# A hybrid attention and state-space layer on one core: a lead before some attention jobs, tables issued sooner, a bank for K0, splits moved to VectorE, gelu in another order and a gated unit with the contraction outside

## The chip, the cores and the metric

The kernel runs on one core of one Trainium2 chip. The metric is the time of one execution on the device in microseconds (us), the median of several runs. A profiled execution gives the trace, from which every row below comes.

## The reference, cut to what matters

One decoder layer over 2048 tokens of width 1024, in float32:

```python
proj = x @ w_in                               # q, k, v, z_a, u, z_s, gate logits
# attention: three groups (window, dilation) = (128,1), (512,4), (2048,16), 8 slots of 64
s = q @ k.T / 8 + alibi; m = s.max(-1); p = exp(s - m); l = p.sum(-1); o = p @ v / l
attn = sum(l * exp(m - m_all) * o) / sum(l * exp(m - m_all)) * silu(z_a)
# state space: 32 groups of 16 channels, 64 complex states each, a scan over the tokens
bu = bb @ u; x_t = ab * x_{t-1} + bu; y = gelu(Re(c @ x_t) + d * u)
y = y * sigmoid(y @ w_glu + b_glu) * silu(z_s)
out = (sigmoid(g_a) * (attn @ w_attn_up) + sigmoid(g_s) * (y @ w_ssm_up)) @ w_o
return layer_norm(2 ** 0.25 * x + out)
```

The output has to be float32 in quality, so each product is made of three: an operand is split in a high half (a rounded copy) and a low half (the rest), and TensorE adds high x high, high x low and low x high.

## The kernel before, in words

Work is written as Python generators that yield after every few matmuls, and the order in which they issue instructions is the order of each engine's queue. `interleave` (L237) mixes a bulk generator (projections, 48 products of 512 columns a block, `BLK`) with a side generator (tables, an attention job, the state-space stage): it takes the side whenever its share of its own total is no larger than the bulk's share. TensorE thus always has bulk products between the side's steps.

The tokens go in two halves of 1024 (h = 0, 1). The stages are:

1. Prologue: the projection of u, then V, Q and K of the first attention job, beside `s5_tables` (L735), some hundreds of small VectorE instructions. Their yields add up to 25.01; the side total given is 29.0, the bulk's is 8 blocks. It ends with five stores of the tables from SP (L926, L928).
2. For each half, four head pairs and three groups: `job_proj` (L346) makes Q, K (and V for even pairs, `v_gemm` L403) and `job_attn` (L519) does the attention of the job before it as the side. Odd pairs have another projection (`za` or `zs`) behind K. Q and K come out of PSUM as two copies of ScalarE (L382) and two subtractions of VectorE (L384). V goes through DRAM: ScalarE stores it, SP loads it (L370), ScalarE copies the high half (L375, issued inside K's product), POOL subtracts (L376). For the third group, the keys of every token block lie in both halves of K's product. The first step of `job_attn` is a bias (L525, VectorE) and `scores(0)`, two products of the two slots (L579) and two more with the low half of Q (L581).
3. The gates (16 for each half, `gate_block` L683, `tanh` by ScalarE at L703) beside `s5` (L984), whose side total is `S5_TOTAL` = 340. For every 4 groups, `setup` builds E and F (VectorE, with two products on POOL, L1012 and L1017), K0 = E x F (L1030, bank `sca`), copies it (L1033, ScalarE), stores it and loads it shifted as MD (L1034, L1043). For every 2 groups, `part_a` (L1087, bank `sca`) makes the scan's input, which ScalarE copies to BR and BI (L1094, L1095; two buffers), `part_b` is the scan, 38 VectorE instructions (L1106 to L1134), and `part_c` (L1153, L1154, bank `scb`) makes y, which goes to DRAM.
4. `yprep` (L1193) loads y of half 1 channel by channel and applies gelu: Square (ScalarE, L1207), a product (VectorE, L1209), Tanh (ScalarE, L1211), a product (L1213), the high half (ScalarE, L1217), the low half (VectorE, L1219), for four blocks, as the last part of the side.
5. `stage_glu` (L1225) multiplies y by w_glu, one output block after another, each in one bank for 512 tokens; the eviction is a tanh (ScalarE, L1240), two products and a low half (VectorE, L1244, L1245, L1252). Then `stage_y`, `stage_c` and the norm, with half 0's gelu beside `stage_c` of half 1.

Weights: `Weights` (L124) has a plan of 128x1024 tiles in the order of use and two raw buffers. `ahead` (two contraction steps into a product) begins the next tile's split: the high half of one 512-column part by ScalarE (L171), the low half by POOL (L172). `ahead2` (six steps in) does the other part and fetches the tile after. The evictions of one product and the start of the next are ordered by the two `proj` banks.

Of the kernel before, what the change touches and what calls it, by code (L numbers as in the profile page):

```python
# [9 lines left out]
F32 = mybir.dt.float32  # L10
F32R = mybir.dt.float32r
# [8 lines left out]
HALF = 1024  # L20
# [21 lines left out]
def layer_kernel(ctx, tc, xT, xnat, w_in, w_v, w_up, w_glu, w_o, bglu, lng, lnb,  # L42
# [81 lines left out]
    class Weights:  # L124
        def __init__(self, plan):
            self.plan, self.raws, self.splits, self.i = plan, [], [], 0
            self.open = False

        def fetch(self, upto):
            while len(self.raws) < min(upto, len(self.plan)):  # L130
# [35 lines left out]
        def part(self, k, i=None):  # L166
            i = len(self.splits) - 1 if i is None else i
            hi, lo = self.splits[i]
            raw = self.raws[i][0]
            c = self.cols(i, k)  # L170
            A.copy(hi[:, c], raw[:, c])  # L171
            (V if i < 2 and not k else P).tensor_tensor(lo[:, c], raw[:, c], hi[:, c].bitcast(F32), op=OP.subtract)  # L172
            self.open = k == 0

        def finish(self):
            if self.open:
# [2 lines left out]
        def take(self):  # L179
            self.split(self.i + 1)  # L180
            self.finish()
            self.i += 1
            return self.splits[self.i - 1]

# [9 lines left out]
    def gemm(wts, nkt, mh, ml, evac, outer=False, w=None, k0=0, banks=None):  # L194
        hi, lo = w or wts.take()
        last = 3 * nkt - 1
        lead = k0 == 0

        def mms(ps, t, kt):
            cols = slice(t * 512, (t + 1) * 512)  # L200
            wc = slice((k0 + kt) * 128, (k0 + kt + 1) * 128)
            for n, (w, m) in enumerate(((hi, mh), (hi, ml), (lo, mh))):
                T.matmul(ps, w[:, wc], m(kt)[:, cols], start=kt == 0 and n == 0, stop=3 * kt + n == last)  # L203

        if outer:
            ps = [ps_tile(*(banks[t] if banks else ("proj", 2))) for t in range(2)]
            for kt in range(nkt):
                for t in range(2):
                    mms(ps[t], t, kt)
                if kt == 1:  # L210
                    wts.ahead()
                if kt == min(5, nkt - 1):
                    wts.ahead2()
                yield 6 * 0.216
            for t in range(2):
                evac(t, ps[t])
            return
        for t in range(2):
            ps = ps_tile("proj", 2)
            for kt in range(nkt):  # L220
                mms(ps, t, kt)
                if kt % 2 == 1:
                    if t == 0 and kt == 1 and lead:
                        wts.ahead()
                    if t == 0 and kt == min(5, nkt - 1) and lead:
                        wts.ahead2()
                    if kt < nkt - 1:
                        yield 6 * 0.216
            evac(t, ps)
            yield 6 * 0.216  # L230
# [3 lines left out]
        return gemm(wts, 8, lambda k: X["h", k], lambda k: X["l", k], evac, outer, banks=banks)  # L234


    def interleave(bulk, bulk_total, side, side_total):  # L237
        b = s = 0.0
        bulk_on = side_on = True
        while bulk_on or side_on:  # L240
            if side_on and (not bulk_on or s / side_total <= b / bulk_total):
                try:
                    s += next(side)
                except StopIteration:
                    side_on = False
            else:
                try:
                    b += next(bulk)
                except StopIteration:
                    bulk_on = False  # L250
# [469 lines left out]
    glu = [w_glu[e] for e in range(2)]  # L720
    up = [w_up[d] for d in range(8)]
    fin_o = [w_o[q, k] for q in range(2) for k in range(4)]
    plan += gate + gate + (glu + up + fin_o) * 2
    wts = Weights(plan)

    def drain(g):
        for _ in g:
# [3 lines left out]


    G = 32

    def s5_tables(sp):  # L735
        yield 0.01
# [183 lines left out]
                 ks[:, :, n, 0], ks[:, :, n, 1], tk)  # L920
        ts(ks[:, :, :, 2], ks[:, :, :, 1], -1.0, OP.mult)

        o = 0
        for t in (Q1, Q2, P1, P2):
            n = t.shape[1] * t.shape[2]
            S.dma_start(tabD[:, o:o + n], t.rearrange("s g k -> s (g k)"))  # L926
            o += n
        S.dma_start(tabD[:, o:], ks.rearrange("s g n w -> s (g n w)"))  # L928

    def s5_views(sp):  # L930
        tab = sp.tile([128, 1472], F32, name="tab")
# [6 lines left out]
    with tc.tile_pool(name="ap", bufs=1) as ap:  # L938
        ub = [u_block(0, b) for b in range(2, 4)]
        interleave(chain([first_blocks(first_x(ap), [u_evac(0, b) for b in range(2)])] + ub  # L940
                         + [job_proj(ap, wts, 0, 0, 0)]), 8 * BLK, s5_tables(ap), 29.0)
        pend = None
        for h in range(2):
            bulk = [u_block(1, b, b == 0) for b in range(4)] if h else []
            n = len(bulk)
            for pair in range(NPAIR):
                for g in range(3):
                    if h or pair or g:
                        bulk.append(job_proj(ap, wts, h, pair, g))
                        n += 2 if pair % 2 else 4  # L950
                    if pair % 2:
                        bulk.append(zs_block(h, pair // 2) if g == 1 else za_block(h, pair - 1 + g // 2))
                        n += 1
                    if pend is None:
                        drain(chain(bulk))
                    else:
                        interleave(chain(bulk), n * BLK, pend, 16.0)
                    pend = job_attn(ap, jobs.pop())
                    bulk, n = [], 0
            if h == 0:  # L960
                raws = []
                for tag, n in (("QA", 1), ("QB", 1), ("cB", 1), ("KC", 2), ("VV", 2), ("og", 1)):
                    t = ap.tile([128, n * HALF], F32, name="xr", tag=tag, bufs={"og": 5, "cB": 1}.get(tag, 2))
                    raws += [t[:, HALF * k:HALF * k + HALF] for k in range(n)]
                part = iter_until(pend, 3.0)
                zs = [zs_block(0, b, b == 3 and "last") for b in range(2, 4)]
                interleave(chain([spread(zs[0], lambda k: S.dma_start(raws[k], xT[1, k]), 1), next_x(1, zs[1], raws)]),
                           1.2 * BLK, part, 3.0)

        def tail():  # L970
            yield from pend
            while fins:
                step_fin()
                yield 1.0
        gates1 = [gate_block(1, d, d == 15 and "last", d < 5) for d in range(16)]
        interleave(chain([zs_block(1, b) for b in range(2, 4)] + gates1[:5]), 7 * BLK, tail(), 34.0)
# [5 lines left out]
    def s5(sp):  # L982
# [16 lines left out]
        def setup(c):  # L999
# [24 lines left out]
            MI = sp.tile([128, GC, 128], F32, name="MI", bufs=3)  # L1024
            MD = sp.tile([128, GC, 128], F32, name="MD", bufs=3)
            for q in range(GC // 4):
                ps = ps_tile("sca")
                for i in range(4):
                    gg = 4 * q + i
                    T.matmul(ps[0:16, i * 128:(i + 1) * 128], E[:, gg, 7, :],  # L1030
# [164 lines left out]
    def yprep(h, pool, tag, w, ring):  # L1195
        c = math.sqrt(0.044715)

        def one(b):
            y = pool.tile([128, HALF], F32, name="ys", tag=f"{tag}{12 + b % ring}")
            S.dma_start(y, yD[b * 128:(b + 1) * 128, :, 64 * h:64 * h + 64])  # L1200
            yield
            yield
            yield
            yf = pool.tile([128, HALF], F32, name=f"yf{b}", tag=f"{tag}{8 + b}")
            y = y.rearrange("c (p n) -> c n p", p=16)
            y3 = yf.rearrange("c (n p) -> c n p", p=16)
            A.activation(y3, y, AF.Square, scale=c)  # L1207
            yield
            V.scalar_tensor_tensor(y3, y3, 1.0, y, op0=OP.add, op1=OP.mult)  # L1209
            yield  # L1210
            A.activation(yf, yf, AF.Tanh, scale=math.sqrt(2.0 / math.pi))  # L1211
            yield
            V.scalar_tensor_tensor(y3, y3, 1.0, y, op0=OP.add, op1=OP.mult)  # L1213
            yield
            hi = pool.tile([128, HALF], F32R, name=f"yh{b}", tag=f"{tag}{b}")
            lo = pool.tile([128, HALF], F32R, name=f"yl{b}", tag=f"{tag}{4 + b}")
            A.activation(hi, yf, AF.Copy, scale=0.5)  # L1217
            yield
            V.scalar_tensor_tensor(lo, yf, 0.5, hi.bitcast(F32), op0=OP.mult, op1=OP.subtract)  # L1219
            Y_[h, b] = (hi, lo, yf)  # L1220

        gens = [one(b) for b in range(4)]
        lag = 2 if ring == 4 else 4
        for k in range(10 + 3 * lag):
            for b in range(4):  # L1225
                if k >= lag * b:
                    next(gens[b], None)
            yield w

    def stage_glu(h, sact, stile, zs):  # L1230
        late = []

        def ev_e(e, box):
# [20 lines left out]
                if t == 1:  # L1254
                    sact.append((box["hi"], box["lo"]))
            return ev
        for e in range(4):
            if e % 2 == 0:
                w = wts.take()
            yield from gemm(wts, 4, lambda k: Y_[h, k][0], lambda k: Y_[h, k][1], ev_e(e, {}), w=w, k0=4 * (e % 2))  # L1260
# [364 lines left out]
```

## Time and profile before

| | us |
|---|---|
| median of 3 runs | 2194.13 (2193.89 to 2194.81) |
| profiled execution | 2197.31 |
| its span, first to last instruction | 2195.5 |
| TensorE busy (matmuls) | 2151.4 |
| VectorE busy | 1210.5 |
| ScalarE busy | 1019.1 |
| POOL busy | 786.9 |
| mean granted clock of TensorE | 0.993 |

PE is TensorE, DVE VectorE, ACT ScalarE, SP the queue that issues most loads; a q behind an engine's name is its sequencer. L12 is a line of the kernel before. The granted clock is a share of 2.4 GHz; its other level, 0.5, is 1.2 GHz. A matmul's end is modelled, so a busy time runs a little over the next one's start.

### The profile page before, as it was taken

How to read it: one execution, taken by the hardware profiler on the slowest of the kernel's cores; microseconds unless marked ns; L12 is line 12 of the kernel's file. 1: busy time of each engine (PE TensorE's matmuls, PEld its weight loads, DVE VectorE, ACT ScalarE, POOL GpSimd, SP SyncE). 2: the span in 40 equal slices, each digit the busy share in tenths (PEclk: the TensorE clock that was granted, in tenths of full speed). 3: DMA queues.
4: the chain of work that ended last, by engine and by line, in shares of the span. 5: the costliest groups of instructions: out<-in, count | busy, mean ns of one | idle time of the engine just before them, and what ended most of it. 6: DMA issues, size and time to landing. Idle time of an engine off the chain costs nothing. (4 is left out here: it accounts for less than half of the span.)

```text
span 2195.5 us, 32253 instructions
## 1 busy us (share of the span) xinstructions
PE 2151.4 (98%) x11440; PEld 1830.0 (83%) x11440; DVE 1210.5 (55%) x3004; ACT 1019.1 (46%) x2355; POOL 786.9 (36%) x647
## 2 busy tenths in 40 slices
PE   9999999999999999999999999999999999999998
PEld 7898888997888998889998888877888778888786
DVE  6644454445543244555444665158988884368725
ACT  3255565555655355565555665233433362243222
POOL 2222253252352234243243352432222124332643
PEclk9999999999999999999999999999999999999999
DMA  6323444343374334434343433554345364443721
GB/s 175 101 78 97 122 125 135 95 122 109 98 216 118 90 107 121 122 97 112 101 132 100 119 106 117 167 172 127 108 147 157 112 220 127 142 126 111 272 87 77
DMA packets 227569, 278.13 MB, mean 127 GB/s; under 512 B 89552, under 2 KB 175440, under 8 KB 227408
## 3 DMA queue, kind: packets, MB, share of 16 engines
q10 hardware_dynamic: 91776, 143.81, 21.3%
q1 hardware_dynamic: 135632, 132.25, 20.4%
q8 instruction: 91, 1.49, 0.3%
q14 instruction: 70, 0.57, 0.1%
HBM read 189.24 MB, written 74.19 MB: 120 GB/s over the span
## 5 line engine op out<-in xcount | busy, mean ns | idle before, releaser
L172 POOL TENSOR_TENSOR wlo<-wraw,whi 128x512 fp32r<-128x512 f32 (+1 forms) x326 | 445.0, 1376 | 676.8 <-ACT whi L171 624.4
L203 PE MATMUL proj<-xh,whi 128*128 128x512 f32 x1600 | 647.5, 405 | 1.6 <-ACT gt L703 1.6
L203 PE MATMUL proj<-xh,wlo 128*128 128x512 f32 x1600 | 630.5, 394 | 0.0
L203 PE MATMUL proj<-xl,whi 128*128 128x512 f32 x1600 | 628.2, 393 | 0.0
L203 PEld LDWEIGHTS proj<-xh,wlo 128*128 128x128 f32 x1600 | 301.6, 189 | 66.1
L203 PEld LDWEIGHTS proj<-xh,whi 128*128 128x128 f32 x1600 | 303.0, 189 | 56.1 <-ACT gt L703 2.3
L203 PEld LDWEIGHTS proj<-xl,whi 128*128 128x128 f32 x1600 | 302.6, 189 | 51.7
L590 ACT ACTIVATE Sx<-Sx,st 128x256 f32<-128x256 f32 (+1 forms) x384 | 182.1, 475 | 277.9 <-DVE st L586 268.8
L617 POOL TENSOR_TENSOR og<-ot 128x128 f32<-128x128 f32 x192 | 88.5, 461 | 531.5 <-DVE ot L616 510.6
L171 ACT CAST whi<-wraw 128x512 fp32r<-128x512 f32 (+1 forms) x328 | 194.9, 619 | 112.7 <-PE ob L1356 39.9
L601 DVE TENSOR_TENSOR PT<-tr,PT 128x512 fp32r<-128x512 f32 (+1 forms) x192 | 118.9, 620 | 221.3 <-ACT PT L600 220.9
L430 PE MATMUL proj<-whi,xh 128*128 128x256 f32 x768 | 222.0, 289 | 2.1 <-DVE KC L384 2.1
L430 PE MATMUL proj<-wlo,xh 128*128 128x256 f32 x768 | 219.3, 286 | 1.1 <-POOL wlo L172 0.8
L430 PE MATMUL proj<-whi,xl 128*128 128x256 f32 x768 | 218.3, 284 | 0.0
L430 PEld LDWEIGHTS proj<-wlo,xh 128*128 128x128 f32 x768 | 148.0, 193 | 3.2 <-POOL wlo L172 3.0
L430 PEld LDWEIGHTS proj<-whi,xh 128*128 128x128 f32 x768 | 147.9, 193 | 2.3 <-issue 2.3
L430 PEld LDWEIGHTS proj<-whi,xl 128*128 128x128 f32 x768 | 147.9, 193 | 0.0
L586 DVE CUSTOM_DVE_ANT_0 Sx<-sca,bias 128x256 f32<-128x256 f32 (+1 forms) x192 | 74.6, 389 | 123.3 <-PE sca L581 119.9
L616 DVE TENSOR_TENSOR ot<-oa,ot 64x256 f32<-64x256 f32 x192 | 81.1, 422 | 78.8 <-ACT ot L614 65.7
L616 DVE TENSOR_TENSOR ot<-ob,ot 64x256 f32<-64x256 f32 x192 | 81.0, 422 | 75.8 <-ACT ot L614 70.2
L598 PE MATMUL tr<-ident,Sx 128*128 128x128 f32 x664 | 109.2, 276 | 0.5
L600 ACT CAST PT<-tr 128x512 fp32r<-128x512 f32 (+1 forms) x192 | 99.6, 519 | 21.3 <-PE tr L598 10.6
(291 smaller groups left out, 3772.5 us busy)
## 6 DMA issues: line engine op xcount, KB each, us to landing
wraw<-in_w_in_dram ACTq DMA_DIRECT2D x102, 512.0 KB
ld<-gD SPq DMA_DIRECT2D x32, 512.0 KB
gD<-gt ACTq DMA_DIRECT2D x27, 512.0 KB
wraw<-in_w_v_dram ACTq DMA_DIRECT2D x24, 512.0 KB
vD<-th ACTq DMA_DIRECT2D x48, 256.0 KB
cB<-coefD SPq DMA_DIRECT2D x48, 256.0 KB
VV<-vD SPq DMA_DIRECT2D x16, 512.0 KB
xr<-in_xT_dram SPq DMA_DIRECT2D x16, 512.0 KB
```

Of the source, the lines that this page charges most:

```text
L171: A.copy(hi[:, c], raw[:, c])
L172: (V if i < 2 and not k else P).tensor_tensor(lo[:, c], raw[:, c], hi[:, c].bitcast(F32), op=OP.subtract)
L203: T.matmul(ps, w[:, wc], m(kt)[:, cols], start=kt == 0 and n == 0, stop=3 * kt + n == last)
L430: T.matmul(o, X[m, kt][:, 128 * i:128 * i + 128], w[half_k][wx][:, wc], start=kt == 0 and n == 0 and t % 2 == 0, stop=kt == 7 and n == 2, ...
L586: V.tensor_tensor_reduce(sx[:, s, lo:], ps2[s][:, lo:256], bias[:, s, lo:], scale=-0.125, scalar=3.0e38, op0=OP.add, op1=OP.min, accum_out ...
L590: A.activation(sx[:, s, lo:], sx[:, s, lo:], AF.Exp, scale=-1.0, bias=st[:, 0, s, c:c + 1], accum_out=st[:, 1, s, c:c + 1])
L598: T.transpose(p3[:, s, b], Sx[i][:, s, b * 128:(b + 1) * 128], ident)
L600: A.copy(PT[:, 0, :, pos], p3[:, :, lo:])
L601: V.tensor_tensor(PT[:, 1, :, pos], p3[:, :, lo:], PT[:, 0, :, pos].bitcast(F32), op=OP.subtract)
L616: V.tensor_tensor(ot[half[s]], O[half[s], s], ot[half[s]], op=OP.add)
L617: P.tensor_tensor(og[pair, g][:, i * 128:(i + 1) * 128], ot[:, 0], ot[:, 1], op=OP.add)
```

## The change

- `interleave` takes a lead: the side starts only when the bulk has done that much. It is 12 products (12 * 0.216) when the bulk is group 0 of an odd pair, so the pending job is the third group of the even pair before it; 0 elsewhere.
- The side total of the tables' `interleave` is 32.0 in place of 29.0, and the five stores are issued after that `interleave`.
- K0's product takes the bank `oa`.
- For 29 tiles (gates 5 to 15 of half 1, the 16 gates of half 0, the two tiles of w_glu), the low halves go to VectorE: they are noted, and issued at contraction steps 3 and 7 of the running product, or when the tile is taken.
- `yprep` works in y's own order: Square, product and Tanh on a second tile without stride, and only the last product writes in token order.
- In half 1, outputs 0 and 1 of the gated unit are made together with the contraction outermost, in the banks `sca`, `scb`, `oa` and `ob`.

```diff
@@ class Weights
+            self.late, self.todo = range(0), []
...
-            (V if i < 2 and not k else P).tensor_tensor(lo[:, c], raw[:, c], hi[:, c].bitcast(F32), op=OP.subtract)
+            def low(eng):
+                eng.tensor_tensor(lo[:, c], raw[:, c], hi[:, c].bitcast(F32), op=OP.subtract)
+            if i in self.late:
+                self.todo.append(low)
+            else:
+                low(V if i < 2 and not k else P)
...
+        def lows(self):
+            while self.todo:
+                self.todo.pop(0)(V)
...
         def take(self):
             self.split(self.i + 1)
             self.finish()
+            self.lows()
@@ def gemm (both orders)
+                if kt in (3, 7):
+                    wts.lows()
...
+                    if t == 0 and kt in (3, 7):
+                        wts.lows()
@@ def interleave
-            if side_on and (not bulk_on or s / side_total <= b / bulk_total):
+            if side_on and (not bulk_on or b >= lead and s / side_total <= (b - lead) / (bulk_total - lead)):
@@
+    late = range(len(plan) + 5, len(plan) + 34)
     plan += gate + gate + (glu + up + fin_o) * 2
     wts = Weights(plan)
+    wts.late = late
@@ prologue
-                         + [job_proj(ap, wts, 0, 0, 0)]), 8 * BLK, s5_tables(ap), 29.0)
+                         + [job_proj(ap, wts, 0, 0, 0)]), 8 * BLK, s5_tables(ap), 32.0)
+        table_store.pop()()
@@ attention
-                        interleave(chain(bulk), n * BLK, pend, 16.0)
+                        interleave(chain(bulk), n * BLK, pend, 16.0, 12 * 0.216 if g == 0 and pair % 2 else 0.0)
@@ setup
-                ps = ps_tile("sca")
+                ps = ps_tile("oa")
@@ yprep
+            u = pool.tile([128, HALF], F32, name="yt", tag=f"{tag}{4 + b}")
+            A.activation(u, y, AF.Square, scale=c)
+            yield
+            V.scalar_tensor_tensor(u, u, 1.0, y, op0=OP.add, op1=OP.mult)
+            yield
+            A.activation(u, u, AF.Tanh, scale=math.sqrt(2.0 / math.pi))
+            yield
             yf = pool.tile([128, HALF], F32, name=f"yf{b}", tag=f"{tag}{8 + b}")
...
+            V.scalar_tensor_tensor(yf.rearrange("c (n p) -> c p n", p=16), pn(u), 1.0, pn(y),
+                                   op0=OP.add, op1=OP.mult)
@@ stage_glu
+        first = 0
+        if h:
+            first = 2
+            w = wts.take()
+            ps = [ps_tile(nm) for nm in ("sca", "scb", "oa", "ob")]
+            for kt in range(4):
+                for i in range(4):
+                    e, t = divmod(i, 2)
...
+                    for n, (a, m) in enumerate(((0, 0), (0, 1), (1, 0))):
+                        T.matmul(ps[i], w[a][:, wc], Y_[h, kt][m][:, cols],
+                                 start=kt == 0 and n == 0, stop=kt == 3 and n == 2)
+                    if i % 2:
+                        if kt == 0 and i == 3:
+                            wts.ahead()
+                        if kt == 1 and i == 3:
+                            wts.lows()
+                        if kt == 2 and i == 3:
+                            wts.ahead2()
+                        if kt < 3:
+                            yield 6 * 0.216
+                    if kt == 3:
+                        ev_e(e, boxes[e])(t, ps[i])
+                        if t:
+                            yield 6 * 0.216
-        for e in range(4):
+        for e in range(first, 4):
```

## Rows read from the trace of the kernel before

**Rows 1.** page part 1: busy time, share of the span, instructions

```profile
PE 2151.4 (98%) x11440; PEld 1830.0 (83%) x11440; DVE 1210.5 (55%) x3004; ACT 1019.1 (46%) x2355; POOL 786.9 (36%) x647
```

**Rows 2.** waits of TensorE over the span

```profile
PE sca L579 <- DVE KC L384: 10.0, 5, 2.1
...
PE sca L1030 <- ACT BI L1095: 4.1, 1, 4.1
```

**Rows 3.** PE: stretch, length, busy us (instructions), clock, DMA share, GB/s

```profile
97.00:113.00 16.00, 11.39 (x62) 0.79 0.30 89
216.00:226.00 10.00, 7.57 (x28) 0.83 0.51 145
513.00:520.00 7.00, 4.58 (x22) 1.00 0.38 124
1490.00:1502.00 12.00, 7.86 (x28) 0.72 0.31 99
1745.00:1752.00 7.00, 5.23 (x24) 1.00 0.17 64
1765.00:1790.00 25.00, 20.80 (x81) 0.93 0.69 216
```

**Rows 4.** timeline of SP, 73 to 109 us

```profile
99.59 0.32 SPq L928 DMA_DIRECT2D tabD<-PT  x1
100.09 0.37 SPq L370 DMA_DIRECT2D VV<-vD  x1
```

**Rows 5.** timeline of ACT, 92 to 108 us

```profile
104.30 1.05 ACT L375 CAST VV<-VV 128x1024 fp32r<-128x1024 f32 x1 [10.26 <-DMA VV<-vD]
105.37 1.17 ACT L382 CAST KC<-proj 64x512 fp32r<-64x512 f32 x2
```

**Rows 6.** timeline of DVE, 82 to 101 us

```profile
83.19 0.68 DVE L384 TENSOR_TENSOR QLa<-proj,QA 64x512 fp32r<-64x512 f32 x1 [7.19 <-ACT QB L382]
...
90.06 1.27 DVE L915 COPY PT<-arena 64x16 f32<-64x16 f32 x1
...
99.60 1.41 DVE L384 TENSOR_TENSOR KC<-proj,KC 64x512 fp32r<-64x512 f32 x2
```

**Rows 7.** chain of waits, all of it: one step

```profile
1372.32 69.40 PE proj L203 x306
```

**Rows 8.** timeline of POOL, 1454 to 1455 us

```profile
1454.22 1.47 POOL L172 TENSOR_TENSOR wlo<-wraw,whi 128x512 fp32r<-128x512 f32 x1 [0.62 <-ACT whi L171]
```

**Rows 9.** timeline of PE, 217 to 220 us

```profile
216.80 0.39 PE L203 MATMUL proj<-xh,wlo 128*128 128x512 f32 x1
219.17 0.33 PE L579 MATMUL sca<-KC,QA 128*128 128x128 f32 x1 [1.98 <-DVE KC L384]
219.94 0.30 PE L579 MATMUL scb<-KC,QB 128*128 128x128 f32 x1 [0.44 <-issue]
```

**Rows 10.** timeline of DVE, 1454 to 1455 us

```profile
1454.20 0.34 DVE L1106 SCALAR_TENSOR_TENSOR zbi<-zbr,tab,zbi 128x128 f32<-128x128 f32 x1
1454.57 1.26 DVE L1106 SCALAR_TENSOR_TENSOR zbr<-zbr,tab 128x128 f32<-128x128 f32 x1
```

**Rows 11.** busy time of all engines, 1416 to 1780 us

```profile
1416.00:1780.00 364.00, 354.11 (x1584) 288.90 (x1582) 284.38 (x695) 145.10 (x286) 95.00 (x69) 0.99 0.47 146
```

**Rows 12.** groups of DVE by line, 1795 to 1812 us

```profile
L1244 DVE SCALAR_TENSOR_TENSOR th<-th,yf 128x512 f32<-128x512 f32 x7 | 5.9, 840 | 0.0
L1245 DVE TENSOR_TENSOR yf<-th,sl 128x512 f32<-128x512 f32 x7 | 4.8, 692 | 0.2
```

**Rows 13.** groups of DVE by line, 1416 to 1780 us

```profile
L1106 DVE SCALAR_TENSOR_TENSOR zbr<-zbr,tab 128x128 f32<-128x128 f32 x112 | 46.5, 415 | 13.1 <-ACT XS L1141 10.8
```

**Rows 14.** groups of ACT by line, 1755 to 1790 us

```profile
L1207 ACT ACTIVATE yf<-ys 128x1024 f32<-128x1024 f32 x4 | 8.2, 2055 | 2.0 <-DMA ys<-yD 2.0
L1211 ACT ACTIVATE yf<-yf 128x1024 f32<-128x1024 f32 x4 | 4.2, 1062 | 3.0 <-DVE yf L1209 3.0
```

**Rows 15.** groups of DVE by line, 1755 to 1790 us

```profile
L1213 DVE SCALAR_TENSOR_TENSOR yf<-yf,ys 128x1024 f32<-128x1024 f32 x4 | 9.2, 2291 | 1.1 <-ACT yf L1211 1.1
```

More of the change, by code (lines that the diff above doesn't have):

```diff
@@ L234, in xgemm, with interleave @@
         return gemm(wts, 8, lambda k: X["h", k], lambda k: X["l", k], evac, outer, banks=banks)
-    def interleave(bulk, bulk_total, side, side_total):
+    def interleave(bulk, bulk_total, side, side_total, lead=0.0):
         b = s = 0.0
@@ L733, in layer_kernel @@
     G = 32
+    table_store = []
     def s5_tables(sp):
@@ L921, in s5_tables, with store @@
         ts(ks[:, :, :, 2], ks[:, :, :, 1], -1.0, OP.mult)
[L923 to L928, printed above, removed]
+        def store():
+            o = 0
+            for t in (Q1, Q2, P1, P2):
+                n = t.shape[1] * t.shape[2]
+                S.dma_start(tabD[:, o:o + n], t.rearrange("s g k -> s (g k)"))
+                o += n
+            S.dma_start(tabD[:, o:], ks.rearrange("s g n w -> s (g n w)"))
+        table_store.append(store)
     def s5_views(sp):
@@ L1203, in one @@
             yield
-            yf = pool.tile([128, HALF], F32, name=f"yf{b}", tag=f"{tag}{8 + b}")
[L1205 to L1213, printed above, removed]
+            u = pool.tile([128, HALF], F32, name="yt", tag=f"{tag}{4 + b}")
[5 more added lines that the diff above has]
+            yield
+            yf = pool.tile([128, HALF], F32, name=f"yf{b}", tag=f"{tag}{8 + b}")
+            pn = lambda ap_: ap_.rearrange("c (p n) -> c p n", p=16)
+            V.scalar_tensor_tensor(yf.rearrange("c (n p) -> c p n", p=16), pn(u), 1.0, pn(y),
+                                   op0=OP.add, op1=OP.mult)
             yield
             hi = pool.tile([128, HALF], F32R, name=f"yh{b}", tag=f"{tag}{b}")
-            lo = pool.tile([128, HALF], F32R, name=f"yl{b}", tag=f"{tag}{4 + b}")
             A.activation(hi, yf, AF.Copy, scale=0.5)
             yield
+            lo = pool.tile([128, HALF], F32R, name=f"yl{b}", tag=f"{tag}{4 + b}")
             V.scalar_tensor_tensor(lo, yf, 0.5, hi.bitcast(F32), op0=OP.mult, op1=OP.subtract)
@@ L1256, in ev_e @@
             return ev
-        for e in range(4):
+        first = 0
+        if h:
+            first = 2
+            w = wts.take()
+            boxes = {}, {}
+            ps = [ps_tile(nm) for nm in ("sca", "scb", "oa", "ob")]
+            for kt in range(4):
+                for i in range(4):
+                    e, t = divmod(i, 2)
+                    wc = slice((4 * e + kt) * 128, (4 * e + kt + 1) * 128)
+                    cols = slice(t * 512, (t + 1) * 512)
+                    for n, (a, m) in enumerate(((0, 0), (0, 1), (1, 0))):
[15 more added lines that the diff above has]
+        for e in range(first, 4):
             if e % 2 == 0:
```

## The prediction, made blind

> **What bounds the kernel.** I read the page first: TensorE is busy 2151.4 us, 98% of the span [rows 1], so outside its first and last microseconds the kernel is its matmuls plus the few places where TensorE stands. So the next view is TensorE's waits: the two largest inside the run are five before the first score of a job (for KC, the split keys) and one before K0's product (for ScalarE's copy BI) [rows 2]. The third is busy time and granted clock in the stretches round these waits [rows 3]. Each stretch loses its idle time and, where the clock falls from 2.4 to 1.2 GHz behind the wait (a mean of 0.72 to 0.93 there), also (1 - clock) x length: 97 to 113 us: 4.61 + 0.21 x 16 = 8.0; 216 to 226: 2.43 + 1.70 = 4.1; 513 to 520: 2.4, the clock stays up; 1490 to 1502: 4.14 + 3.36 = 7.5; 1745 to 1752: 1.8; 1765 to 1790: 4.2 + 1.75 = 5.9. The stretch at 216 has two more of its kind, behind the third group of each half's even pairs. That makes 8.0 + 3 x 4.1 + 2.4 + 7.5 + 1.8 + 5.9 = 37.9 us that a change of order could give back. Everything else is matmuls, which the change leaves as they are.
>
> The profiled execution took 2197.31 us: 2195.5 of span and 1.8 around it, 3.2 above the median of the runs, 2194.13 (2193.89 to 2194.81). The sum is made against 2197.31 and then taken from 2194.13. About 0.2%, 4.4 us, is what a measurement of this kernel can tell from no change.
>
> **Sooner tables, stores later.** Before, SP has the tables' last store ahead of the load of V; it goes out at 99.59 and V's load at 100.09 [rows 4]. ScalarE waits 10.26 us for that V, and the copy of the second half of the first keys stands behind it until 105.37 [rows 5]; the next job's products stand for that bank, the second wait of this stretch. The first one is the first score's: VectorE works the last piece of the tables from 90.06 on, and only at 99.60 splits the first half of the keys [rows 6]. The yields of the tables add up to 25.01, so the last piece is issued at 25.01/29 of the bulk before and 25.01/32 after: 6.7 units of 82.9 sooner, inside the product of Q's first half and no longer behind Q. VectorE stood 7.19 us before 83.19 [rows 6], so the 9.5 us of this piece run from 76.0 to at most 85.5, and Q's first split ends by 86.9 instead of 84.6. Its bank is wanted 5.4 us (24 products of 0.227, [rows 7]) after Q's first half ended, which is ScalarE's pair of copies (1.17, [rows 5]) before 83.19, so at 87.4: no wait, by 0.5 us. Behind the five stores nothing stands on SP but the first job's saves of keys and V; V's load goes ahead. Both waits and both falls go. What comes next is the second weight tile of V for group 1: its split is issued behind the exponentials of the first score, which need VectorE's two bias products. That wait is between 0 and two halves on POOL (1.47 each, [rows 8]), 2.9; I take 1.1, since four groups of 12 products at half width, 1.4 us each, hide most of it. Gain 8.0 - 1.1 = 6.9.
>
> **Lead.** With group 0 of an odd pair as bulk, the pending job is the third group of the even pair: its first score needs both halves of the keys, and nothing lies between their last product and the score. Before, TensorE stands 1.98 us for the first slot and 0.44 for the second [rows 9]. After, 12 products of Q, 12 x 0.227 = 2.72 us [rows 7], go first; they need a bank whose keys were evicted 5 us earlier and weights that are already split. The second slot's keys are ready 3.14 us after the issue of the last product (216.80 to 219.94, [rows 9]); it will be asked for at 0.23 + 2.72 + 0.12 = 3.07. That is a draw: between 0 and 0.4 per place may remain. The attention job starts 2.6 units later and ends at 29.3 of 31.1 instead of 29.2: nothing behind it moves. Gain 3 x 4.1 + 2.4 = 14.7, less 0.1.
>
> **K0's bank.** K0 takes the bank of the scan's input product, which ScalarE copies out (BI) only when VectorE has freed BR and BI. With "oa", free in this stage except for gate 15 of the second half (no K0 is issued inside it), TensorE goes on at 1491. K0's copy keeps its place on ScalarE, so its DMAs leave no later. What is late next is the scan's next input product, which still needs BI; it is issued a whole scan later (38 VectorE instructions of 0.34, [rows 10], 13 us). Gain 7.5, bounds 4 to 7.5.
>
> **Splits on VectorE.** 29 weight tiles, 58 halves. On POOL a half takes 1.47, and a VectorE instruction that meets it takes 1.26 instead of 0.34 [rows 8, 10]: 0.92 lost. VectorE is busy 284.38 of 364 us here, 78% [rows 11], so about 58 x 0.78 x 0.92 = 42 us return, and 58 x 0.69 (128x512 with two inputs, [rows 12]) = 40 us are added: even for VectorE's sum. A split now queues behind the scan, and ScalarE's fetch of the tile after next waits for VectorE to have read the raw tile. A half is issued after 12 or 24 products of the running tile and used after 24 of the other half or later, 5.4 us or more; one level of the scan is four instructions of a mean 0.42, 1.7 us [rows 13]. Three levels of lag would be hidden: cost 0, bounds -2 to +6. The 1.8 us at 1747, where TensorE waits for the scan's last states, I count as gone, since POOL no longer takes VectorE's turns ahead of it (two halves, 1.8 us).
>
> **Gelu and gated unit.** Four blocks go through Square, product, Tanh, product, two halves. In y's order Square reads without stride: 1.06 as Tanh does, not 2.06 [rows 14]. The first product, which had the stride of the second, falls to at most 1.4 (twice a 128x512 of 0.69, [rows 12]); the second still writes with a stride, between 1.4 and its 2.29 [rows 15], and I take 2.0, as no row shows a stride on one side alone. A block's turn (Square, first product, Tanh) falls from about 5.4 to 3.9 at most, so the last of four blocks is ready some 4 to 6 us sooner. The unit needs block 0 alone at its start and the others 2.7, 5.4 and 8.2 us later, on four banks that wait for no gate. So the 5.9 us go. The added price: four evictions fall due within 2.1 us of each other, each 0.84 + 0.69 + a low half of 0.69 = 2.2 us on VectorE [rows 12], 8.9 in all, and the second half of the second gate weight's split is issued behind them. TensorE meanwhile has 24 products of outputs 2 (5.5 us) before outputs 3 need it, and the first eviction starts 2.1 us before the four banks end: 8.9 - 2.1 - 5.5 leaves 1.3, of which ScalarE's overlap hides some; I take 0.9, bounds 0 to 3.
> The Trainium skill, Perfetto Trace Analysis, section Optimizing Tensor Performance, speaks against this order: matmul groups should rotate through banks so that one's evacuation overlaps the next group's products. By that rule all 8.9 us would show and the sum would be 8 us worse, 2166; by the rows the next output's products cover most of it, and no run here shows the four together.
>
> **Sum.** 6.9 + 14.6 + 7.5 + 1.8 + 5.9 - 0.9 = 35.8. 2197.31 - 35.8 = 2161.5 for the profiled execution, 2194.13 - 35.8 = 2158 for the median.
>
> **Rivals.** (a) *Waits move on instead of going.* Each removed wait hands TensorE to the next thing on VectorE's queue: 0.4 for the second slot at four places with the clock falling at three (1.6 + 5.1 = 6.7), 3.5 of K0's on BI, 1.8 more in V's weights with one fall of 1.7, 1.8 at the last states. That leaves 35.8 - 15.5 = 20 and gives 2174. For: the draw and the margin of 0.5 us above, and clock falls behind waits of 2 us. Against: most margins are over 2 us. (b) *Slower: late low halves.* If VectorE is one level, 1.7 us, too late at each of the 29 tiles, 29 x 1.7 = 49 us come in: 2158 + 49 = 2207. It decides from 1.2 us per tile (35.8/29), 1.4 for slower by over 0.2%. For: if the 42 us do not return, VectorE needs 284 + 40 = 324 of 354, and its waits for DMAs must fit in what is left. Against: rows 8 and 10 show the return, and the issue is at least 5.4 us ahead. (c) *Nothing much.* The waits are hidden by something the view doesn't tell, as TensorE's ends are modelled: within 4 us, 2192. Against: the granted clock, which is not modelled, falls right behind them.
>
> **Numbers.** Forecast 0.74, (a) 0.18, (b) 0.05, (c) 0.03. Forecast alone reaches from 37.9 plus 4 of small waits (2152) to 27 gained (2167); with (a) the range is 2152 to 2174, which leaves out (b), (c) and small ends. Faster 0.92, same 0.03, slower 0.05.
>
> **What would show it.** After: no TensorE wait of over 0.5 us for KC; clock 1.00 in the first 1200 us behind the start; V's load on SP ahead of the table stores; no K0 wait on BI; VectorE's scan instructions near 0.34 except beside E's products; y's last half ready before the unit asks. Wrong if TensorE waits on VectorE's wlo between 1416 and 1780, or if the clock falls at new places.

## The result, and the profile after

The changed kernel takes 2167.14 us (median of four runs, 2166.24 to 2168.37), the kernel before, beside it, 2194.47 (2193.89 to 2195.64): a ratio of 0.9876, with a 95% interval of 0.9861 to 0.9891. So 27.3 us went, where 36 were forecast: inside the range of 2152 to 2174, 9 us above the number, and at the upper end of the 2152 to 2167 that the forecast had for itself. The profiled execution took 2166.73 us, 30.6 under that of before (2197.31).

The page's first part, after; TensorE's row answers to [rows 1]:

```profile
span 2164.9 us, 32185 instructions
...
PE 2137.0 (99%) x11440; PEld 1822.8 (84%) x11440; DVE 1191.7 (55%) x3062; ACT 1007.4 (47%) x2355; POOL 704.2 (33%) x589
```

The number of products is the same. The span is 30.6 us shorter in two nearly equal parts: TensorE stands 2164.9 - 2137.0 = 27.9 us where it stood 44.1 (16.2 less), and the same products keep it busy 14.4 us less, most of it because the clock falls far more rarely: the falls in [rows 3] and at the two other places like 216 make 13.6 us, those after the change 1.6.

Waits of TensorE, after (engine, line, waited for: us in total, times, longest), against [rows 2]:

```profile
PE tr L614 <- ACT Sx L606: 5.1, 4, 1.3
PE proj L215 <- ACT th L1263: 4.2, 1, 4.2
PE proj L215 <- ACT gt L719: 1.2, 1, 1.2
```

Neither the waits for KC nor the 4.1 us for BI are there. In their place stand four waits of 1.2 to 1.3 us for ScalarE's exponentials (Sx) ahead of a transposition, and one of 4.2 us in the gated unit for ScalarE's Tanh (th). The third row was there before.

TensorE by stretch, after (stretch, length, busy us and instructions, clock, DMA share, GB/s); the first, second, fourth and fifth are the places of the first, second, fourth and fifth line of [rows 3]:

```profile
94.00:110.00 16.00, 16.00 (x121) 1.00 0.20 62
205.00:215.00 10.00, 10.00 (x47) 1.00 0.32 104
238.00:248.00 10.00, 8.66 (x42) 1.00 0.22 55
1465.00:1477.00 12.00, 12.00 (x59) 1.00 0.40 127
1718.00:1724.00 6.00, 6.00 (x28) 1.00 0.27 93
...
1758.00:1776.00 18.00, 13.82 (x54) 0.91 0.58 209
```

The old places are full, at the full clock. The third row is a new place behind a lead: 1.3 us. The last is the gated unit: 4.2 us of standing and 0.09 x 18 = 1.6 of clock, 5.8 in all, where the last line of [rows 3] lost 5.9. So of the 37.9 us counted before, 32.0 went and 5.9 were replaced by 5.8; four new waits took 5.1. That leaves 27.0 of the 30.6. The other 3.6 were not itemized. Set against the first product behind the scan (1749.91 us before, 1720.95 after; experiment 3 has these rows), 2.1 of them came ahead of it, 0.9 from there to the end of the gated unit, and 0.7 later (rounded).

### The profile page after: what moved, and what is told of

Read it like the earlier page. It is cut to its first block, busy times and chain, and to the rows that moved or that the text cites. A ratio compares the mean times of both kernels' runs of the same rounds, so it can differ in the third digit from the quotient of the medians.

```text
span 2164.9 us, 32185 instructions
## 1 busy us (share of the span) xinstructions
PE 2137.0 (99%) x11440; PEld 1822.8 (84%) x11440; DVE 1191.7 (55%) x3062; ACT 1007.4 (47%) x2355; POOL 704.2 (33%) x589
## 5 line engine op out<-in xcount | busy, mean ns | idle before, releaser
L175 POOL TENSOR_TENSOR wlo<-wraw,whi 128x512 fp32r<-128x512 f32 (+1 forms) x268 | 357.1, 1343 | 530.7 <-ACT whi L172 508.9
L400 DVE TENSOR_TENSOR KC<-proj,KC 64x512 fp32r<-64x512 f32 x96 | 66.1, 689 | 82.9 <-ACT KC L398 81.6
```

What stands on the lines that cost most here:

```text
L175: eng.tensor_tensor(lo[:, c], raw[:, c], hi[:, c].bitcast(F32), op=OP.subtract)
```

## The experiments

All are the changed kernel with one edit, unless told otherwise, and are set against its 2167.14 us. The kernel before, run beside each of them, took 2192.93 to 2195.81 us, and each ratio has an interval of about 0.0015, 3 us, on either side. So a difference of less than some 4 us between two medians is not told by the medians; there the argument rests on the waits in the traces, each of a single execution.

### 1. The lead: is it the source of the four new waits?

Three edits of one line, the call that paces an attention job (16.0) and holds it back (12 products):

```
-  interleave(chain(bulk), n * BLK, pend, 16.0, 12 * 0.216 if g == 0 and pair % 2 else 0.0)
+  e_lead0:        ... 16.0, 0.0
+  e_lead12_slow:  ... 15.3, 12 * 0.216   (at these places)
+  e_lead24:       ... 16.0, 24 * 0.216   (at these places)
```

> The changed kernel with the lead taken back to 0, all else kept. Theory (the lead removes the waits for the split keys and itself makes the four new waits of 1.2 us for the exponentials at 242, 535, 900 and 1209 us): the waits of 2 us for KC come back at four places, with the clock at half behind three of them, and the waits for the exponentials are gone: 14.7 - 5.1 = 9.6 us slower than the changed kernel, some 2176.5 us. Rival (the waits for the exponentials come from another part of the change): they stay beside the returned ones: 14.7 us slower, some 2182 us.

> The lead of 12 products is kept, but the attention steps are paced to end with the bulk (15.3 in place of 16 in the pace), which puts 108 products between the first score and the last transposes where the changed kernel has 102 and the kernel before 114. Theory (squeezed steps: ScalarE and VectorE fall behind, step by step, until TensorE waits for the last exponentials): the four waits fall from 1.2 us to under 0.4, the time to some 2162 to 2164 us. Rival (the split of V on ScalarE, 1.05 us, in the middle of the job makes the wait, whatever the pace): the four waits stay over 0.9 us, 2167 us.

> The lead doubled to 24 products: the ten steps share 120 products in place of 132. Theory (squeezed steps): the waits for the exponentials stay, or grow beyond 1.2 us and come at more steps: 2167 to 2175 us. Rival (only the place counts: in the changed kernel the eviction of the keys falls 6 products before the last score; here it falls 12 products before it): the waits vanish, 2162 us.

Measured: 2175.08, 2163.09 and 2179.60 us (ratios to before 0.9914, 0.9862, 0.9937; intervals 0.9900 to 0.9929, 0.9847 to 0.9876, 0.9921 to 0.9954). TensorE's waits without the lead:

```profile
PE sca L595 <- DVE KC L400: 7.9, 4, 2.0
...
PE scb L595 <- issue: 1.7, 4, 0.4
```

With the slower pace:

```profile
PE ob L625 <- DVE PT L617: 2.0, 4, 0.6
```

And with the doubled lead:

```profile
PE sca L595 <- DVE st L602: 7.8, 13, 1.2
...
PE oa L625 <- DVE PT L617: 2.3, 4, 0.8
```

The lead removes the waits for KC and makes those for Sx: without it they change places. The slower pace lands inside its forecast of 2162 to 2164 us, though its waits stay a little over the 0.4 expected; its rival falls, as V's split still stands in the middle of the job. The rival by place falls with the doubled lead, which should have been free of waits and is slower than no lead at all, by 4.5 us. There the theory had only the direction: it allowed 2175 us at most. Of the 12.5 us that the doubled lead costs, 6.5 are standing of TensorE; the rest was not followed. What orders the variants is how densely the steps follow: between the second score and the last transposes the program has 96 products before the change, 84 after it, 90 with the slower pace, and the waits there are none, 1.2 to 1.3 us, and 0.4 to 0.6. With 24 products the count is 84 too, and the step ahead of it has also lost 6.

How this looks at one place, in the changed kernel. ScalarE, 233 to 243 us (start, duration, instruction, in brackets the idle time before it and what ended it):

```profile
234.14 1.05 ACT L391 CAST VV<-VV 128x1024 fp32r<-128x1024 f32 x1
235.21 0.75 ACT L630 COPY ot<-ob 64x256 f32<-64x256 f32 x2
237.33 0.40 ACT L606 ACTIVATE Sx<-Sx,st 128x128 f32<-128x128 f32 x1 [1.37 <-DVE st L602]
...
238.37 1.18 ACT L398 CAST KC<-proj 64x512 fp32r<-64x512 f32 x2
239.57 0.74 ACT L630 COPY ot<-oa 64x256 f32<-64x256 f32 x2
...
242.27 0.40 ACT L606 ACTIVATE Sx<-Sx,st 128x128 f32<-128x128 f32 x1 [1.31 <-DVE st L602]
```

VectorE and TensorE at the same place:

```profile
239.58 1.39 DVE L400 TENSOR_TENSOR KC<-proj,KC 64x512 fp32r<-64x512 f32 x2 [0.65 <-ACT KC L398]
240.98 0.86 DVE L632 TENSOR_TENSOR ot<-oa,ot 64x256 f32<-64x256 f32 x2
241.87 0.29 DVE L602 CUSTOM_DVE_ANT_0 Sx<-sca,bias 128x128 f32<-128x128 f32 x1
```

```profile
235.60 0.40 PE L625 MATMUL oa<-PT,VV 128*128 128x256 f32 x2
...
237.29 0.33 PE L595 MATMUL sca<-KC,QA 128*128 128x128 f32 x1
...
242.81 0.72 PE L614 MATMUL tr<-ident,Sx 128*128 128x128 f32 x2 [1.23 <-ACT Sx L606]
```

The last score starts at 237.29, and VectorE takes it up only at 241.87, 4.6 us later, behind the low halves of the new keys (239.58) and an earlier step's output (240.98). That one waits for ScalarE, which copies the output, done on TensorE at 235.60 + 0.40, at 239.57, 3.6 us late: behind the keys (238.37), the exponentials (237.33) and, before them, V (234.14). Neither engine is full; each waits for the other, step by step, and with 84 products they have no break in which to catch up.

### 2. The lead for the first score alone

```
-  if side_on and (not bulk_on or b >= lead and s / side_total <= (b - lead) / (bulk_total - lead)):
+  if side_on and (not bulk_on or b >= lead and s / side_total <= b / bulk_total):
```

> The lead holds back the first score alone: behind it the attention steps stand where they stood before the change (paced by the whole bulk, not by what the lead leaves of it). Theory (squeezed steps): no wait for the split keys and none over 0.4 us for the exponentials at the four places: 5.1 us less standing, 2162 us, and better than the pace of 15.3, which left four waits of 0.5 us. Rival (with only 6 products between the first score and the second step, the first transposes now wait): four waits of about 1 us at the first transposes, 2165 to 2167 us.

Measured: 2160.80 us (2160.25 to 2161.43), ratio 0.9842 (0.9826 to 0.9858). The steps behind the first score are at 96 products again. The stretch of both places above, 200 to 250 us, is full:

```profile
200.00:250.00 50.00, 50.00 (x255) 1.00 0.42 125
```

The changed kernel has 48.66 us of products there. None of TensorE's waits at the four places is left above 0.25 us, and the first transposes, 6 products behind the first score, do not wait. So the lead is good as far as it serves the first score; the squeeze of the others was its price.

### 3. The gated unit: what holds TensorE for 4.2 us?

ScalarE of the changed kernel at this place, with the DMA that it issues (ACTq):

```profile
1763.75 0.62 ACT L1273 CAST sh<-yf 128x512 fp32r<-128x512 f32 x1 [0.78 <-DVE yf L1268]
1764.28 1.13 ACT L172 CAST whi<-wraw 128x512 fp32r<-128x512 f32 x2
1768.41 0.34 ACTq L137 DMA_DIRECT2D wraw<-in_w_up_dram  x1
1768.80 0.69 ACT L1263 ACTIVATE th<-proj,bgl_h 128x512 f32<-128x512 f32 x1 [3.38 <-POOL wlo L175]
```

And VectorE, POOL and TensorE there:

```profile
1765.51 1.75 DVE L1275 TENSOR_TENSOR sl<-yf,sh 128x512 fp32r<-128x512 f32 x1
1767.18 1.74 DVE L175 TENSOR_TENSOR wlo<-wraw,whi 128x512 fp32r<-128x512 f32 x1
```

```profile
1764.97 3.41 POOL L175 TENSOR_TENSOR wlo<-wraw,whi 128x512 fp32r<-128x512 f32 x2 [112.39 <-ACT whi L172]
```

```profile
1769.54 0.79 PE L215 MATMUL proj<-yh,whi 128*128 128x512 f32 x1 [4.18 <-ACT th L1263]
```

Outputs 3 need the bank of outputs 2, which ScalarE's Tanh reads; the Tanh stands behind the fetch of a weight tile, which goes out only when POOL has ended two splits. Beside it, the second half of the second gate weight's low part, queued behind the four evictions on VectorE, ends at 1768.9. Four edits:

```
  e_fetch_sp:   that one fetch is issued on SP, not on ScalarE
  e_low_early:  wts.lows() behind wts.ahead2() at kt == 2, ahead of the four evictions
  e_both:       both
  e_unit_old:   the unit one output and bank at a time, as before the change
```

> In the second half's gated unit the one fetch of the next weight tile that is issued beside outputs 2 goes out on SP in place of ScalarE. Theory (ScalarE stood 3.4 us at that issue for POOL's split, with the Tanh of outputs 2 behind it; and the second half of the second gate weight's low part, on VectorE behind the four evictions at 1767.2 to 1768.9, is late by nearly as much): the Tanh starts some 3.4 us sooner, but TensorE then waits for the low part: the 4.2 us at outputs 3 shrink by only 0.5 to 1.5, the clock still falls: 2166 us. Rival (ScalarE's issue is the only cause): TensorE stands 0.9 us or less and the clock stays up: 5 us faster, 2162 us.

> The second half of the second gate weight's low part is given to VectorE ahead of the four evictions, not behind them; the fetch stays on ScalarE. Theory (two waits side by side): ScalarE still stands for POOL's split, so the wait at outputs 3 stays between 3 and 4.2 us: 2166 to 2167 us. Rival (the low part on VectorE is what counts): the wait is 1 us or less, 2162 us.

> Both edits: the fetch on SP and the low part ahead of the evictions. Theory (two waits side by side): the wait at outputs 3 falls from 4.2 us to about 1, the clock stays up behind it: 3.2 + 1.7 = 5 us faster than the changed kernel, 2162 us. Rival (the four evictions that fall due together are the bound, 8.9 us of VectorE against 5.5 us of products): the wait stays over 2.5 us, 2165 us or more.

> The gated unit of the second half as before the change, one output and bank at a time; gelu keeps y's order. What it tells: whether taking the contraction outside pays. Theory (it pays less than its jam costs, since y's last block comes only 2 to 3 us after the gates end): TensorE waits 1 to 2.5 us for y at the unit's start, with or without a fall of the clock, and not at outputs 3: 2163 to 2167 us. Rival (the order with the contraction outside is needed): TensorE waits over 4 us in the unit, 2168 us or more.

Measured: 2165.90, 2162.86, 2162.48 and 2164.24 us (ratios 0.9874, 0.9858, 0.9857, 0.9865, each with about 0.0015 on either side). With the fetch on SP, TensorE at outputs 3:

```profile
1765.64 0.50 PE L216 MATMUL proj<-yh,whi 128*128 128x512 f32 x1 [0.60 <-ACT th L1264]
...
1768.59 0.49 PE L216 MATMUL proj<-yh,wlo 128*128 128x512 f32 x1 [2.23 <-DVE wlo L176]
```

The Tanh is on time, 0.6 us, and the late low half takes over, as the theory had it. With the low half early, on ScalarE:

```profile
1765.30 0.34 ACTq L137 DMA_DIRECT2D wraw<-in_w_up_dram  x1
1765.70 1.14 ACT L172 CAST whi<-wraw 128x512 fp32r<-128x512 f32 x2
1766.74 0.68 ACT L1263 ACTIVATE th<-proj,bgl_h 128x512 f32<-128x512 f32 x1
```

The wait at outputs 3 is 1.4 us and the clock stays at 1.00. Here the theory of two independent waits fell, and the rival came nearest (it had said 1 us or less): the fetch now goes out at 1765.30, before POOL has begun (1766.39). The built program shows why. There are two raw weight buffers, and in the changed kernel the fetched tile was given the one that POOL was just splitting, since the older one still had its low half to be read; with that half early it gets the older one and waits for nothing on POOL. The trace of the changed kernel agrees: the fetch goes out at 1768.41, behind POOL's end (1764.97 + 3.41 = 1768.38) but 0.5 us ahead of the end of the low half that still reads the older buffer (1768.92). So the one late low half held both: its own product and, through the buffer, the fetch, ScalarE behind it, and the evictions. The fetch on SP adds nothing to that (2162.48 against 2162.86). With both edits the wait is 1.2 us, so the rival of the four evictions as the bound (over 2.5 us, 2165 us or more) falls.

The old order of the unit, with gelu in y's order, loses 1.2 us for y's high half and 0.8 for its low one, and no clock, as its theory had it. TensorE over the same 217 products, from the last gates to the first product of the next stage: before the change, after it, with the old order, and with the low half early (columns as above; the first is the stretch, the second its length; the counts take in instructions that the ends of the stretch cut):

```profile
1749.91:1806.62 56.71, 52.51 (x218) 0.97 0.70 218
```

```profile
1720.95:1776.69 55.74, 51.56 (x218) 0.97 0.71 222
```

```profile
1722.03:1774.36 52.33, 50.39 (x219) 1.00 0.76 236
```

```profile
1721.63:1773.18 51.55, 50.12 (x219) 1.00 0.76 240
```

The faster gelu takes 4.4 us out of this stretch (together with the splits of its tiles on VectorE, which no run here takes apart from it); as built, the four banks together gave back 3.4 of them. With the low half early they add 0.8 to the gelu's gain. These are single profiles: the medians, 2164.24 and 2162.86 us, do not tell the two orders apart.

### 4. Splits, K0's bank, tables: each undone alone

```
  e_splits_pool: - wts.late = late
  e_k0_sca:      ps = ps_tile("oa") -> ps_tile("sca")
  e_tables_old:  s5_tables(ap), 32.0 -> 29.0; the five stores issued at once
```

> The changed kernel with the low halves of the 29 gate and gate-unit tiles on POOL again, as before. Theory (VectorE gains as much from POOL's silence as it gives for the splits; the wait for the scan's last states goes because of the splits): VectorE's scan instructions go back to a mean of 0.41 us, the wait of 1.8 us for XS near the stage's end comes back, and the low half behind the evictions is gone with it: between 1 us faster and 2 us slower than the changed kernel, and the 4.2 us at outputs 3 shrink. Rival (the splits on VectorE are the source of a gain that the waits don't show): 4 us or more slower.

> The changed kernel with K0's product back in the bank of the scan's input. Theory (K0's bank is worth what the wait of before cost): one wait of about 4 us for BI in the stage, with the clock at half behind it: 6.6 to 7.5 us slower than the changed kernel, 2174 us. Rival (with the splits off POOL, VectorE frees BI sooner and the bank no longer matters): within 2 us of the changed kernel, 2167 to 2169 us.

> The changed kernel with the tables paced and stored as before (29 in place of 32, the five stores issued at once). Theory: the waits of 2 us for the split keys come back near 98 and 106 us with the clock at half behind both; the 0.7 us at 14 us, where VectorE's splits of the first x stand among the sooner tables, go: 8.5 - 0.7 = 7.8 us slower, some 2175 us. Rival (the wait at 14 us has nothing to do with the tables): it stays, 8.5 us slower.

Measured: 2170.57 (2168.48 to 2171.43), 2170.46 (2168.26 to 2173.41) and 2177.04 us (2176.36 to 2177.14); ratios 0.9894, 0.9900, 0.9925 (intervals 0.9880 to 0.9909, 0.9883 to 0.9916, 0.9911 to 0.9939). TensorE's waits with the splits on POOL:

```profile
PE oa L1051 <- DVE F L1042: 3.5, 1, 3.5
PE scb L1175 <- DVE XS L1155: 1.7, 1, 1.7
...
PE proj L215 <- ACT th L1262: 0.6, 1, 0.6
```

The stretch of its first row, and with the splits on VectorE but K0 in its old bank the wait that answers to it:

```profile
1500.00:1514.00 14.00, 10.48 (x39) 0.76 0.36 112
```

```profile
PE sca L1052 <- ACT BI L1117: 1.8, 1, 1.8
```

So the two parts share one gain. K0's bank alone, with POOL splitting, trades the wait for BI (7.5 us with its clock) for one for F, which VectorE makes: 3.5 + 0.24 x 14 = 6.9. The splits alone bring BI's wait from 4.1 to 1.8 with no fall of the clock. By these traces the bank by itself is worth 0.6, the splits by themselves 5.7, both 7.5. In the gated unit the wait is 0.6 without the late low half, so undoing the splits costs 3.5 + 3.4 + 1.7 and gives 3.6 + 1.6 back: 3.4 net, as the medians have it. Both theories missed. The first allowed 2 us at most; what it had left out is the wait for F, not a gain that the waits don't show. The second wanted 6.6 to 7.5 us; the medians say 3.3, over a wide spread, the profiled executions 1.5 (2168.26 against 2166.73). That median lies outside the rival's 2167 to 2169 too. The one trace is of the fastest of its four runs and has the rival's mechanism in part, a wait of 1.8 us where there were 4.1, and no fall of the clock behind it; what the slower three had is not shown. So how the 7.5 us divide between bank and splits rests on single traces; by the medians, undoing either costs the same.

VectorE's own time is not even: it is less with the splits. All engines over the same work, from the clearing of the scan's first tiles to the first product behind its last, with the splits on VectorE and then with them on POOL (behind the length: busy us and instructions of PE, PEld, DVE, ACT, POOL):

```profile
1396.00:1720.95 324.95, 323.59 (x1467) 265.40 (x1466) 255.38 (x735) 125.79 (x267) 25.09 (x16) 1.00 0.46 145
```

```profile
1397.30:1729.79 332.49, 325.53 (x1461) 265.83 (x1460) 266.41 (x685) 125.11 (x266) 88.17 (x66) 0.99 0.45 142
```

With 50 instructions more, VectorE is busy 11.0 us less. From 1390 to 1745 us both kernels have it busy for 272 us, but by the end of the scan the one that splits on POOL is 8.8 us behind, so the same stretch of time holds less of its work. One kind of the scan's instructions (behind the first bar its busy us and the mean ns of one) with the splits on POOL, and after:

```profile
L1127 DVE SCALAR_TENSOR_TENSOR zbr<-zbi,tab,zbr 128x128 f32<-128x128 f32 x112 | 44.7, 399 | 0.0
```

```profile
L1128 DVE SCALAR_TENSOR_TENSOR zbr<-zbi,tab,zbr 128x128 f32<-128x128 f32 x112 | 38.4, 343 | 0.0
```

With the tables as before the waits for KC near 98 and 107 us come back (2.0 + 0.4, and 1.0), with the clock at 0.79 from 97 to 113 us, as in [rows 3]:

```profile
97.00:113.00 16.00, 11.96 (x66) 0.79 0.27 83
```

The time is 9.9 us longer, 2 more than expected. The waits near 14 us stay (2.1 us in all), so the rival was right there: they are not the tables' doing. They are between 0 and 2.3 us in the profiles of this study and were not followed.

### 5. Three edits together

```
  the pace of 2; wts.lows() as in e_low_early; the first gate's two halves in banks ob and proj
```

> Three edits on the changed kernel together: the lead for the first score alone, the low half of the second gate weight ahead of the evictions, and the first gate's two halves in two different pairs of banks (ob and proj), so that the second gate does not stand for ScalarE's two copies (1.15 us near 1550). Theory (the waits are apart in time and none is the cover of another): the gains add: 6.3 us (first score alone) + 4.3 (low half) + 1.2 = 11.8 us under the changed kernel, 2155 to 2156 us. Rival (they overlap, or ob's bank meets another use): over 2158 us.

Measured: 2156.79 us (five runs, 2155.80 to 2157.41), ratio 0.9831 (0.9817 to 0.9844): 10.4 under the changed kernel. The waits:

```profile
PE proj L215 <- ACT th L1264: 1.3, 1, 1.3
PE ob L215 <- ACT gt L719: 1.0, 1, 1.0
```

The first two gains add, 6.3 + 4.3 = 10.6. The third edit gave nothing: the wait for gt only moved to the start of that gate, whose bank ob the gate before still holds (1.0 for 1.15). That is why the time lies 0.8 us above the 2155 to 2156 expected. It is the fastest of all.

## Why the prediction was right or wrong

The total stands because what was read as lost was lost, and most of it was removable. By the profiled executions, 35.8 us were forecast and 30.6 came. The lead was short by 5.0 and the gated unit by 4.9; the tables' price of 1.1, which was not due, and the 3.6 that no term had counted cover 4.7 of that. So the total came nearer than its terms, and that much of it is luck. The rest of the 9 us is the step from the profiled execution to the median: I took the whole sum from 2194.13, though the profiled run lay 3.2 above it. After the change it lies 0.4 under its median. So the 3.2 look like a part of what went, not a constant on top; no second trace of the kernel before shows where they lay.

**Tables: right, the added price not due.** Forecast 8.0 - 1.1; the stretch now loses nothing, and no wait for V's weights came. V's load leaves SP at 79.09, ahead of the five stores (79.57 to 85.24), and Q's first split ends at 85.81 + 0.69 = 86.5, where 86.9 was worked out.

**Lead: the gain right, a price missed.** The waits went, second slots included, whose draw fell to nothing. The step that failed is "ends at 29.3 of 31.1 instead of 29.2: nothing behind it moves". I looked at where the job ends and not at the pace in between: 84 products where there were 96. Price 5.1 us. Experiments 1 and 2 show it and take it away.

**K0: the sum right, the credit wrong.** 7.5 us went, as forecast, but the step named the scan's next input product as what is late next. It is VectorE's F, 3.5 us and a fall of the clock, which shows as soon as the splits are on POOL again. By the traces of experiment 4, most of the term came with the splits.

**Splits: right, and better than even.** The prediction set 42 us of return against 40 of splits; VectorE is 11.0 us less busy. There was no wait of TensorE for a low half in the scan's stage, and XS's wait is gone. The one low half that came late is the last of the 29, in the unit.

**Gelu and gated unit: the failed step that cost most.** Forecast were 5.9 won and 0.9 (0 to 3) paid, 5.0 in all; the stretch of the unit and the last gates is 1.0 shorter, since the 5.9 went, 5.8 came, and 0.9 more went that was not itemized. The durations were right or nearly so: Square 1.06, first product 1.22 (at most 1.4 was said), second 1.97 (2.0). I also had the low half behind the evictions. What I left out was the weight tile's fetch on ScalarE between two evictions: that DMA waited at its issue for POOL and held the Tanh behind it, 3.4 us. The term for the jam itself was too small as well: with the fetch out of the way TensorE still stands 0.6 + 2.2 us, and the clock falls.
By the Trainium skill, DMA: Bandwidth & Descriptors, section Anatomy of one DMA — SWDGE (gpsimd) path, a semaphore is waited for on the issuing sequencer before the dispatch. That section is on DMAs issued from GpSimd; this one is issued on ScalarE, and the trace agrees for it: the issue at 1768.41 follows POOL's end at 1768.38, and the Tanh comes right behind it. The rule of the Trainium skill that the prediction weighed (Perfetto Trace Analysis, section Optimizing Tensor Performance) gave 2166 and was nearer than my term, but by luck: the four banks are not what held TensorE: with the low half early they are still evicted together, and the wait is 1.4 us, not 8.9.

**Rivals.** (a) had the kind right, waits that move on, and 2174 was 7 us too slow; none of the places that it named was one of those that came. (b) and (c) had no part: no tile's low half in the scan's stage was late, and the clock did not fall until 1769 us. That fall is one of the two signs of being wrong that the prediction named, a fall at a new place, and it marks the term that failed. The signs of being right came: no wait for KC, no wait of K0 for BI, V's load ahead of the stores, y ready when the unit asked.

## What to carry to other kernels

When work is held back, count what the rest of it must now be done within: a lead that squeezes a chain of two engines pays for itself in the last step. Where a split or a copy is put off, follow its source buffer too: the late reader decides which buffer the next load gets and who waits at its issue. And a removed wait belongs to the part without which the next one in line shows; only undoing each part alone tells which that is.

## What was not expected

The same wait does not always bring the clock down. Without the lead four places have the same 2.4 us of standing, and the clock fell behind two of them; in the kernel before, behind three. These rows are 502 to 512 and 866 to 876 us without the lead:

```profile
502.00:512.00 10.00, 7.58 (x28) 0.83 0.44 133
866.00:876.00 10.00, 7.63 (x37) 1.00 0.24 78
```

Nor is the fall always as long: behind 4.18 us of standing in the gated unit the changed kernel has a clock of 0.91 over 18 us, 1.6 us lost; behind 4.41 at the same place the kernel with the slower pace has 0.81, 3.4 lost. By my estimate from these rows, the clock term of a single profile is uncertain by a few times 1.7 us, which is the size of the 3.2 above.

VectorE and POOL slow each other when both work: in the gated unit POOL's two splits take 1.7 us each, where the median of its splits after the change is 1.29, and beside them VectorE's instruction of 0.69 takes 1.74 to 1.75. Which of the two waits for the other was not tried.
